# Second score product of the 64-wide heads over all 128 rows of the array

## The chip, the cores and the metric

The kernel runs on one core of one Trainium2 chip. The metric is the device time of one execution in microseconds. TensorE (PE, with its weight loads listed apart as PEld), VectorE (DVE), ScalarE (ACT), GpSimd (POOL) and SyncE (SP, which issues the transfers) each run their own instructions in order and wait for one another through semaphores.

## What is computed

The reference is two blocks on 256 tokens of width 1024. The first block has two layers; each layer norms latents and context, projects them with one wide matrix, runs three attention branches and sums them with gates. The second block has four mixers and is not touched here. What matters are the scores of two of the branches, whose heads are 64 wide:

```python
def diff_attend(q, k, v, lam):
    s = jnp.einsum('bqhmd,bkhmd->bhmqk', q * (DIFF_HD ** -0.5), k)
    p = jax.nn.softmax(s.astype(jnp.float32), axis=-1)
    a = (p[:, :, 0] - lam * p[:, :, 1]).astype(v.dtype)
    return jnp.einsum('bhqk,bkhd->bqhd', a, v)
...
def swa_context(q, k, v, sink):
    ...
    (p,) = sink_softmax(sink, (jnp.einsum('bqhgd,bkhd->bhgqk', qg, k),))
```

The differential branch has 8 heads of two 64-wide maps each, the sliding-window branch 16 heads of 64. All in float32.

## The kernel before, in words

Every float32 operand of a product is cut into two parts, a first (high) part and a second (low) part that is the rest, and a product is the sum of three matmuls: high by high, high by low, low by high (`mm3`, lines 101 to 103, most of the kernel's matmuls). The 64-wide heads use a shorter way. `pairs` (line 661) turns a query tile into one tile per half of the 128 partitions: the half that holds the head has its high part, the other half its low part. `twice` (line 673) does the keys: the high part of a head stands on both halves of a tile, and one more tile, `lo`, holds the low parts, each on its own half alone. So `scores` makes one score tile from two matmuls: line 850 over all 128 rows (high by high and low by high at once), and line 854 over the 64 rows of the head (high by low). Between them, for the sliding window's latents, line 853 adds the mask by a matmul with the identity. The heads of the differential branch get their keys from `twice` in `heads_t` (lines 646 to 659: four transposes into a PSUM bank of the kind `tp`, of which there are two), the first head of a unit while the unit before it is still in attention, the second head at the start of `diff_att`. The sliding window's keys already stand twice in the tile (`swa_keys`), so that `parts` gives both parts on both halves.

A layer runs its three branches in units of 256 columns, four to a branch; the projections of the next unit (many matmuls of lines 101 to 103) are put between the attention steps of a unit. The order on each engine is set by a scheduler at build time, from priorities by program order, and the slots of a pool are given out by it as they come free. The tiles of `pairs`, `twice` and the values are all of the kind `ut`, which has 12 buffers in the first layer and 15 in the second.

After the scores the row maximum is taken on DVE (lines 877 and 879), the exponential on ACT (line 882), the scaling on DVE (line 894), the turning on PE (line 903), and the product with the values on PE (lines 919 and 994).

Of the kernel before, what the change touches and what calls it, by code (L numbers as in the profile page):

```python
# [19 lines left out]
F32 = mybir.dt.float32  # L20
# [8 lines left out]
# Buffers of a kind: of the weights as loaded and in parts, of PSUM's banks, and of the first block's tiles  # L29
# by layer. Tiles of a kind are given out in the order of the program.  # L30
BUFS = dict(raw=3, w=4, start=12, mm=3, sc=2, tp=2, av=1, ut=(12, 15), yb=(26, 40), sz=4, pe=4, pt=2, st=2, tmp=2)
# How far ahead of their place in the program (or, if less than nothing, behind it) instructions are scheduled
# [3 lines left out]
class Core:  # L36
    """Buffers and the steps that every layer uses."""
# [28 lines left out]
    @contextmanager  # L66
    def shifted(self, ahead):
        """Instructions that are scheduled ahead of their place, and leave the others' as it is"""
        at = self.tc.cur_priority
        self.tc.cur_priority = max(0, at - ahead)  # L70
        yield
        self.tc.cur_priority = at

    # ---- float32 as the exact sum of two float32r parts
# [4 lines left out]
    def weights(self, src, k, f, stream=None):  # L79
        """A chunk of weights as granules [128, k, f], each with its two parts."""  # L80
        return [self.granule(src[g], k, f, stream) for g in range(src.shape[0])]
# [13 lines left out]
    def mm3(self, out, a, b, start, stop, ahead=False):  # L95
        """out += a.T @ b, with a and b as pairs of parts."""
        nc, tc = self.nc, self.tc
        at = tc.cur_priority
        if ahead:
            tc.cur_priority = max(0, at - AHEAD)  # L100
        nc.tensor.matmul(out, a[0], b[0], start=start, stop=False)  # L101
        nc.tensor.matmul(out, a[0], b[1], start=False, stop=False)  # L102
        nc.tensor.matmul(out, a[1], b[0], start=False, stop=stop)  # L103
        if ahead:
            tc.cur_priority = at + 3

    def gemm_n(self, out, h, cols, grans, k0=0, start=True, stop=True):
        """out [tokens, features]: the tokens' columns of h held, the weights moved."""
        ks = [(hi[:, k, :], lo[:, k, :]) for hi, lo in grans for k in range(hi.shape[1])]
        for k, w in enumerate(ks):  # L110
            a = (h[0][:, k0 + k, cols], h[1][:, k0 + k, cols])
            self.mm3(out, a, w, start and k == 0, stop and k == len(ks) - 1, True)

    def gemm_2(self, out, a, grans):
        """out += a.T @ weights, for columns of a that hold whole numbers or parts of them"""
        tc, nc = self.tc, self.nc
        ks = [g[i][:, k, :] for g in grans for k in range(4) for i in range(2)]
        at = tc.cur_priority
        for j, w in enumerate(ks):
            tc.cur_priority = max(0, at + j - AHEAD)  # L120
            nc.tensor.matmul(out, a[:, j // 2], w, start=j == 0, stop=j == len(ks) - 1)  # L121
        tc.cur_priority = at + len(ks)

    def gemm_t(self, out, gran, h, cols, k0=0, start=True, stop=True):
        """out [features, tokens]: the weights held, the tokens moved."""
        hi, lo = gran
        n = hi.shape[1]
# [4 lines left out]
    def rstd(self, pool, ss, n, name="rstd"):  # L132
        """(sum + n eps) ** -0.5: the root of n is left to the gain."""
        w = ss.shape[1]
# [10 lines left out]
    # ---- rows of tokens: their mean squares by blocks, and what is normed from them  # L145
    def squares(self, x, ss, i, width=256):
        """ss[:, i] = the sum of the squares of a block of x, over 1024"""
# [10 lines left out]
    def norm_turn(self, pool, xg, r, shift, h, cols_of, second=None):  # L158
        """h[:, k, cols] = parts of (xg r + shift).T, with the gain already in xg, but for the second
        half where its rows and gain are given"""  # L160
# [32 lines left out]
def silu2(c, work, p, shape_like=None, bufs=2):  # L193
    """2 silu(z) of z in PSUM, [128, n]."""
# [8 lines left out]
def out_gemm(c, x, w, yT, nk, gain):  # L203
    """x[t] += (y @ w) / 2; with the next norm's gain, the rows times it and their roots"""
# [107 lines left out]
def mixer_b(c, x, rs, P, i):  # L312
    nc = c.nc
    with ExitStack() as st:
        h = normed(c, rs, i)
        work = st.enter_context(c.pool(f"wb{i}", bufs=2))
        # gains: as columns past the rotary part, in the rotary tables within it
# [186 lines left out]
# ---- layouts on the host  # L504
def pack_k(np, w, f=256):
    """w [K, N], f columns at a time, cut along K: [N // f, K // 128 / k, 128, k, f], f k = 1024."""
# [5 lines left out]
def pack_f(np, w):  # L512
    """w [K, N], 256 columns at a time, cut along N: [N // 256, 2, 128, K // 128, 128]."""
# [50 lines left out]
class Hybrid:  # L564
    """A layer of the first block. Token tiles 0, 1 are latents and 2, 3 context."""
# [11 lines left out]
    def setup(self, pool, work):  # L577
        """Small tables of the layer."""
# [47 lines left out]
    def gemm_pair(self, grans, grp, n):  # L626
        """[128, 2, n] of the two token tiles of a group."""
# [6 lines left out]
    # ---- rotary: rows of heads [128, 2, heads, 2 * half]  # L634
# [11 lines left out]
    # ---- heads: parts of the transposes of stages [128, 2, width] by group  # L646
# [14 lines left out]
    def pairs(self, p, n):  # L661
        """For each half of the rows of p, its two parts as the halves of the rows of one tile: the
        number's own half has its first part, the other half the second."""
# [9 lines left out]
    def twice(self, p, n):  # L673
        """For each half of the rows of p, its first part on both halves of a tile; and the second parts."""
        nc = self.c.nc
        out = []
        lo = self.ut()
        for own, other in HALVES:
            t = self.ut()
# [3 lines left out]
            out.append(t)  # L683
        return out, lo

    # ---- latent attention
    def mla_prep(self):
# [7 lines left out]
        def rows(n):  # L695
            """Rows of the two token tiles of a group, and the sums of the squares of their parts"""
# [21 lines left out]
        def turned(src, grp, dst, gain, nk):  # L718
            """transposes with the gain, in parts"""
# [49 lines left out]
    def mla_proj(self, un):  # L769
        """Keys [nope | rotary twice] and queries [nope | x cos | x turned sin] of two heads, turned; the  # L770
        rotary part comes first in the second head."""
# [54 lines left out]
    def z_unit(self, r, un):  # L826
        """2 silu(z) of 256 columns, turned: two tiles [128, nt]"""
# [12 lines left out]
    def scores(self, p, q, k, half, grp, t, keys, mask=False):  # L840
        """q and k as parts; for a half q as tiles from pairs, and k's first part on both halves"""
# [6 lines left out]
        else:  # L848
            rows = HALVES[half][0]
# [4 lines left out]
            nc.tensor.matmul(p, q[half][rows, qs], k[1][rows, ks], start=False, stop=True)  # L854

    def softmaxes(self, q, k, half, grp, neg=None, sink=None):
        """Rows of probabilities [128, keys] of the group's two tiles; with neg, their negative
        lambda-fold factors besides, and not scaled."""
# [8 lines left out]
    def softmax(self, q, k, half, grp, ts, keys, neg, sink):  # L867
        """of tiles that share a bank"""
# [28 lines left out]
    def turned_p(self, ps, kts):  # L897
        """Parts of the transposes of two rows of probabilities, at two key tiles: [128 keys, 2, 256]"""
# [11 lines left out]
    def apply(self, out, ps, keys, v, both=None):  # L910
        """out [dv, 256 queries] = (p @ v).T"""
# [9 lines left out]
    def y_out(self, av, sz, col=None):  # L921
        """The branch's y silu(z) (twice), turned, in parts."""
# [12 lines left out]
    # ---- differential attention  # L935
    def qk_stage(self, gr, grp, heads, q, name):
        """[128, 2, heads * 64] after the rotation; the queries scaled."""
# [81 lines left out]
    # ---- sliding window  # L1019
    def swa_keys(self, su):  # L1020
        """Keys of two groups of heads, each twice, for the two halves of the partitions; and values, as their
        two parts side by side."""
# [20 lines left out]
        return [(((hi, hi), lo), v) for (hi, lo), v in zip(kt, vt)]  # L1043
# [10 lines left out]
    def swa_att(self, un, made, ahead):  # L1054
        """and what ahead() makes between its halves"""
# [23 lines left out]
    # ---- sum over the branches  # L1079
    def gates(self, r, dd, tile):  # L1080
        """tanh of half the gates"""
# [11 lines left out]
    def merge(self, r, parts):  # L1093
        """Parts of 256 columns of the sum over the branches; the last branch leaves its parts."""
# [31 lines left out]
    def run(self, K, h):  # L1126
        """The three branches, four units each; a unit's projections come before the attention of the one
        before it is through, and the sum over a branch goes along with the next one."""
# [30 lines left out]
# The parts of the sum over the branches that follow a branch's first units, by layer  # L1159
MERGE = (((0, 1, 2, 3),), ((0,), (1,), (2,), (3,)))  # L1160
# The steps of the modulation that go along with a branch's sum, by layer
# [5 lines left out]
class ModStart:  # L1167
    """The first layer's gain and shift, 256 columns at a time, for the rows of load_mixed: the latents'
    on the first half of the partitions, the context's on the others."""
# [23 lines left out]
class ModRows:  # L1193
    """Rows of the modulation, for the latents and the context, kept in DRAM: shift, gain with the
    norm's, and a quarter of the gate, for the two halves left out of silu and sigmoid."""
# [5 lines left out]
    def step(self, l, i, cc):  # L1201
        """256 columns of part i of layer l"""
# [19 lines left out]
    def row(self, l, i, pool, both):  # L1222
        """The row on all partitions, or the latents' on half of them and the context's on the others"""
# [7 lines left out]
def hybrid_out(c, P, l, xs, m, G, pool, xg, gain, done, first=None):  # L1231
    """xs += gate (merged @ w_out), xg = xs times the gain, and done(t, mean squares by blocks) as a
    tile is; with the gain after that, xs is times the gain (and done has its mean squares) and xg
    times both."""
# [29 lines left out]
def load_mixed(c, xp, P):  # L1264
    """Four tiles, each of 64 latents and 64 rows of context."""
# [6 lines left out]
def first_block(c, stack, P):  # L1272
    """The latents' rows, normed, as two tiles, and the sums of their squares."""
# [5 lines left out]
    with ExitStack() as st:  # L1279
# [60 lines left out]
        for l in range(2):  # L1340
# [8 lines left out]
            with c.pool(f"merged{l}", bufs=1, side="right") as mp:  # L1349
# [5 lines left out]
                with c.pool(f"tail{l}", bufs=1) as w:  # L1355
# [11 lines left out]
                    else:  # L1367
# [5 lines left out]
                        def done(t, ss, s2):  # L1373
                            """The two norms' roots: 1 / sqrt(s2 / (ss + eps) + eps) / sqrt(ss + eps)"""
# [106 lines left out]
```

## Time and profile before

| | us |
|---|---|
| median of 3 runs | 2538.19 |
| lowest and highest | 2535.25, 2541.75 |
| the profiled execution, span | 2537.5 |
| PE busy in it | 2494.2 |
| DVE, ACT, POOL busy | 1724.8, 1294.1, 155.7 |

The page gives each engine's busy time; a matmul's record has a modelled end, and matmuls overlap, so the length of a record says little of what it costs the engine. The start of a matmul to the start of the next one is what the engine spends on it. A row of the timeline gives start and length in us, the engine, the line, the tiles as out<-in and a form: "128\*128" is rows by columns of the array in use, "128x512" the partitions and columns that are moved through.

### The profile page before, as it was taken

To read this page: it belongs to the slowest core of one execution; us is meant where nothing else is said; L and a number is where in the kernel's file an instruction comes from. 1 tells how busy PE (TensorE), PEld (TensorE's weight loads), DVE (VectorE), ACT (ScalarE), POOL (GpSimd) and SP (SyncE) were. 2 spreads that over 40 slices of the span, in tenths; PEclk is the share of its full clock that TensorE was granted. 3 is DMA by queue.
4 is the path that set the end of the run, shared out by engine and by line. 5 is a ranking of instruction groups with operands and counts; after the bars stand their busy time and mean duration, and the time that the engine had idled before them with its cause. 6 is when DMAs were issued, how large, how long until landed. Compare 5 with 4: busy or idle time off the path is not lost.

```text
span 2537.5 us, 43544 instructions
## 1 busy us (share of the span) xinstructions
PE 2494.2 (98%) x17352; PEld 2276.2 (90%) x17352; DVE 1724.8 (68%) x3073; ACT 1294.1 (51%) x2566; POOL 155.7 (6%) x162
## 2 busy tenths in 40 slices
PE   9999999999999989999999999999999999999999
PEld 7889888888888868999999999999889998898998
DVE  4675655677747864686777888667667776685675
ACT  3554544555535553464555667454455555454643
POOL 0000011000010100210000000010000000000000
PEclk9999999999999999999999999999999999999999
DMA  6222244221232114323333433565554454455554
GB/s 251 77 71 67 63 139 149 67 67 50 84 122 71 58 50 148 102 92 100 117 117 117 142 101 116 200 192 174 167 180 149 152 156 132 158 183 192 175 168 148
DMA packets 91149, 321.40 MB, mean 127 GB/s; under 512 B 11641, under 2 KB 12481, under 8 KB 90945
## 3 DMA queue, kind: packets, MB, share of 16 engines
q1 hardware_dynamic: 90946, 318.62, 38.8%
q8 instruction: 136, 2.23, 0.4%
q14 instruction: 67, 0.55, 0.1%
HBM read 316.45 MB, written 2.13 MB: 126 GB/s over the span
## 4 chain that ended last, share of the span: by engine, by line
PE 95%; DVE 2%; ACT 1%; DMA 1%; issue 0%; POOL 0%; SPq 0%; ACTq 0%; POOLq 0%; DVEq 0%
PE mm L101 25%; PE mm L103 25%; PE mm L102 25%; PE sc L854 3%; PE tp L903 3%; PE av L919 3%; PE sc L850 2%; PE av L994 1%; PE mm L1188 1%; PE mm L121 1%; PE sc L103 1%; PE sc L102 1%; PE sc L101 1%; PE tp L653 1%; DVE wlo L77 1%; ACT whi L76 1%
## 5 line engine op out<-in xcount | busy, mean ns | idle before, releaser
L77 DVE TENSOR_TENSOR wlo<-raw,whi 128x1024 fp32r<-128x1024 f32 (+1 forms) x564 | 687.1, 1220 | 362.4 <-ACT whi L76 357.0
L76 ACT CAST whi<-raw 128x1024 fp32r<-128x1024 f32 (+1 forms) x564 | 586.6, 1043 | 664.7 <-PE mm L102 346.3
L101 PE MATMUL mm<-whi,hhi 128*128 128x256 f32 x2016 | 578.8, 288 | 4.1 <-ACT hhi L76 3.3
L103 PE MATMUL mm<-whi,hlo 128*128 128x256 f32 x2016 | 577.8, 288 | 2.0 <-DVE bgc L321 1.0
L102 PE MATMUL mm<-wlo,hhi 128*128 128x256 f32 x2016 | 575.5, 286 | 0.0
L103 PE MATMUL mm<-hhi,wlo 128*128 128x256 f32 (+1 forms) x1608 | 501.2, 313 | 0.0
L102 PE MATMUL mm<-hlo,whi 128*128 128x256 f32 (+1 forms) x1608 | 500.3, 312 | 0.0
L101 PE MATMUL mm<-hhi,whi 128*128 128x256 f32 (+1 forms) x1608 | 499.6, 312 | 0.0
L101 PEld LDWEIGHTS mm<-whi,hhi 128*128 128x128 f32 x2016 | 386.4, 192 | 11.5 <-ACT hhi L76 4.3
L103 PEld LDWEIGHTS mm<-whi,hlo 128*128 128x128 f32 x2016 | 385.2, 191 | 11.9 <-issue 8.3
L102 PEld LDWEIGHTS mm<-wlo,hhi 128*128 128x128 f32 x2016 | 386.5, 192 | 6.3 <-issue 5.1
L102 PEld LDWEIGHTS mm<-hlo,whi 128*128 128x128 f32 x1608 | 307.3, 191 | 16.6 <-issue 2.0
L103 PEld LDWEIGHTS mm<-hhi,wlo 128*128 128x128 f32 x1608 | 307.3, 191 | 16.6 <-issue 1.5
L101 PEld LDWEIGHTS mm<-hhi,whi 128*128 128x128 f32 x1608 | 307.1, 191 | 16.0 <-issue 1.2
L882 ACT ACTIVATE pe<-sc,sst 128x512 f32<-128x512 f32 (+1 forms) x240 | 147.5, 617 | 122.4 <-DVE sst L877 75.4
L101 PE MATMUL mm<-yb,whi 128*128 128x512 f32 (+1 forms) x440 | 152.3, 349 | 4.7 <-ACT yb L76 3.7
L102 PE MATMUL mm<-yb,whi 128*128 128x512 f32 (+1 forms) x440 | 151.7, 345 | 0.8 <-DVE yb L77 0.8
L103 PE MATMUL mm<-yb,wlo 128*128 128x512 f32 (+1 forms) x440 | 151.4, 344 | 0.0
L77 DVE TENSOR_TENSOR ptl<-tp,pth 128x512 fp32r<-128x512 f32 x160 | 108.0, 684 | 27.2 <-ACT pth L76 18.3
L76 ACT CAST pth<-tp 128x512 fp32r<-128x512 f32 x160 | 91.1, 587 | 63.9 <-PE tp L903 51.4
L877 DVE TENSOR_REDUCE sst<-sc 128x1 f32<-128x512 f32 (+1 forms) x120 | 81.8, 686 | 46.3 <-PE sc L854 32.2
L903 PE MATMUL tp<-ident,pe 128*128 128x128 f32 x640 | 102.1, 275 | 0.8 <-DVE ptl L77 0.8
(320 smaller groups left out, 4081.1 us busy)
## 6 DMA issues: line engine op xcount, KB each, us to landing
raw<-in_b_qkv_dram SPq DMA_DIRECT2D x72, 512.0 KB
raw<-in_a_uz_dram SPq DMA_DIRECT2D x64, 512.0 KB
raw<-in_win_z_dram SPq DMA_DIRECT2D x48, 512.0 KB
raw<-in_win_d_dram SPq DMA_DIRECT2D x48, 512.0 KB
raw<-in_win_g_dram SPq DMA_DIRECT2D x48, 512.0 KB
raw<-in_wbr_dram SPq DMA_DIRECT2D x48, 512.0 KB
raw<-in_w_mod_dram SPq DMA_DIRECT2D x32, 512.0 KB
raw<-in_a_v_dram SPq DMA_DIRECT2D x32, 512.0 KB
```

The lines of the kernel that those rows point to most:

```text
L76: self.nc.scalar.copy(hi, src)
L77: self.nc.vector.tensor_sub(lo, src, hi.bitcast(F32))
L101: nc.tensor.matmul(out, a[0], b[0], start=start, stop=False)
L102: nc.tensor.matmul(out, a[0], b[1], start=False, stop=False)
L103: nc.tensor.matmul(out, a[1], b[0], start=False, stop=stop)
L121: nc.tensor.matmul(out, a[:, j // 2], w, start=j == 0, stop=j == len(ks) - 1)
L850: nc.tensor.matmul(p, q[half][:, qs], k[0][half][:, ks], start=True, stop=False)
L854: nc.tensor.matmul(p, q[half][rows, qs], k[1][rows, ks], start=False, stop=True)
L877: nc.vector.tensor_reduce(st[:, 0], p, axis=AX, op=OP.max, negate=True)
L882: nc.scalar.activation(e[:, i], p[:, i], AF.Exp, bias=st[:, 0, i:i + 1], accum_out=st[:, 1, i:i + 1])
L903: nc.tensor.transpose(p[:, i * 256 + t * 128:i * 256 + t * 128 + 128], ps[t][:, kt * 128:kt * 128 + 128], c.ident)
L919: c.nc.tensor.matmul(out, w, p, start=lo + j + i == 0, stop=lo == 1 and j == nk - 1)
```

## The change

`twice` now makes a low-part tile for each half, as it already did for the high part: the low part on its own half as before (DVE, line 682), and a copy of it on the other half by GpSimd. It returns two lists. `scores` makes the second product over all 128 rows, from the same query tile as the first, and the caller of the sliding window passes its low-part tile for both halves. With the query's low part on the other half the second product now adds low by low as well. Comments and docstrings are taken out, which moves the lines below by two.

```diff
     def twice(self, p, n):
...
         nc = self.c.nc
-        out = []
-        lo = self.ut()
+        his, los = [], []
         for own, other in HALVES:
-            t = self.ut()
+            t, lo = self.ut(), self.ut()
             nc.scalar.copy(t[own, :n], p[own, :n])
             nc.scalar.copy(t[other, :n], t[own, :n].bitcast(F32))
             nc.vector.tensor_sub(lo[own, :n], p[own, :n], t[own, :n].bitcast(F32))
-            out.append(t)
-        return out, lo
+            nc.gpsimd.tensor_copy(lo[other, :n], lo[own, :n].bitcast(F32))
+            his.append(t)
+            los.append(lo)
+        return his, los
...
         else:
-            rows = HALVES[half][0]
             nc.tensor.matmul(p, q[half][:, qs], k[0][half][:, ks], start=True, stop=False)
             if mask:
                 o = p[:, 128:256] if t == 0 else p[:, 0:128]
                 nc.tensor.matmul(o, self.K["ident"], self.K["swa_mask"][:, t], start=False, stop=False)
-            nc.tensor.matmul(p, q[half][rows, qs], k[1][rows, ks], start=False, stop=True)
+            nc.tensor.matmul(p, q[half][:, qs], k[1][half][:, ks], start=False, stop=True)
...
-        return [(((hi, hi), lo), v) for (hi, lo), v in zip(kt, vt)]
+        return [(((hi, hi), (lo, lo)), v) for (hi, lo), v in zip(kt, vt)]
```

The scheduler moves instructions by a few places. Three places matter below. First TensorE, at the first scores of the first differential unit of layer 0 (`tp` is the bank of the turned keys, `sc` the scores, `ut` the tiles of queries and keys, `mm` the projection of the unit that follows). Before:

```order
L653 MATMUL tp_2682<-ident_61,st_k_2292 128x128
L653 MATMUL tp_2682<-ident_61,st_k_2292 128x128
L653 MATMUL tp_2682<-ident_61,st_k_2347 128x128 x2
L850 MATMUL sc_2709<-ut_2595,ut_2608 128x512
L854 MATMUL sc_2709<-ut_2594,ut_2608 128x512
L103 MATMUL mm_2974<-whi_2969,hlo_80 128x256
```

and after the change:

```order
L653 MATMUL tp_2685<-ident_61,st_k_2292 128x128
L653 MATMUL tp_2685<-ident_61,st_k_2292 128x128
L653 MATMUL tp_2685<-ident_61,st_k_2347 128x128 x2
L852 MATMUL sc_2715<-ut_2594,ut_2611 128x512
L856 MATMUL sc_2715<-ut_2595,ut_2611 128x512
L102 MATMUL mm_2980<-wlo_2970,hhi_79 128x256
```

The sequence is the same, four matmuls earlier; the two score matmuls still stand side by side, with projection matmuls behind them.

Second VectorE, in the same unit, where the low parts of the second head's two key tiles are made (line 682; 669 is the same step of its queries). Before, both stand between the first two row maxima:

```order
L877 TENSOR_REDUCE sst_2711<-sc_2709 128x1
L682 TENSOR_TENSOR ut_2687<-tp_2682,ut_2688 64x512
L877 TENSOR_REDUCE sst_2720<-sc_2718 128x1
L886 RECIPROCAL sst_2711<-sst_2711 128x1
L682 TENSOR_TENSOR ut_2687<-tp_2682,ut_2692 64x512
```

After, the first stands there still, and the second is here, 16 rows further on:

```order
L986 SCALAR_TENSOR_TENSOR pe_2735<-pe_2744,sst_2745,pe_2735 128x512
L879 TENSOR_REDUCE sst_2794<-sc_2792 128x2
L682 TENSOR_TENSOR ut_2697<-tp_2685,ut_2696 64x512
L669 TENSOR_TENSOR ut_2707<-tp_2702,ut_2707 64x512
L879 TENSOR_REDUCE sst_2807<-sc_2805 128x2
```

It now stands one row ahead of the first of the two L669 of the same head, which has kept its place; the scheduler had a `ut` slot for it only there.

Third GpSimd, at the start of the differential branch (L789 are copies for the branch before, `dr` a root of the branch's norm, `modrow` a row of the modulation). Before:

```order
L789 CAST ut_1917<-km0_428 64x512
L789 CAST ut_1918<-km1_429 64x512
L142 TENSOR_TENSOR dr_3415<-dre_3413,mhalf_70 128x8
L1213 TENSOR_TENSOR modrow_3606<-modrow_3606,modlow_3609 2x256
L1213 TENSOR_TENSOR modrow_3645<-modrow_3645,modlow_3648 2x256
```

and after:

```order
L791 CAST ut_1917<-km0_428 64x512
L791 CAST ut_1918<-km1_429 64x512
L683 CAST ut_2595<-ut_2595 64x512
L683 CAST ut_2601<-ut_2601 64x512
L683 CAST ut_2691<-ut_2691 64x512
L683 CAST ut_2697<-ut_2697 64x512
L142 TENSOR_TENSOR dr_3424<-dre_3422,mhalf_70 128x8
L683 CAST ut_3332<-ut_3332 64x512
L683 CAST ut_3338<-ut_3338 64x512
L1215 TENSOR_TENSOR modrow_3615<-modrow_3615,modlow_3618 2x256
```

The new copies (L683) stand in units of two ahead of and behind the roots; there are 32 in the program. The order of the transfers on SyncE is the same as before.

## Rows read from the trace of the kernel before

**Rows 1.** The page: span, engines (busy, share, instructions), the chain that ended last by engine.

```profile
span 2537.5 us, 43544 instructions
...
PE 2494.2 (98%) x17352; PEld 2276.2 (90%) x17352; DVE 1724.8 (68%) x3073; ACT 1294.1 (51%) x2566; POOL 155.7 (6%) x162
...
PE 95%; DVE 2%; ACT 1%; DMA 1%; issue 0%; POOL 0%; SPq 0%; ACTq 0%; POOLq 0%; DVEq 0%
```

**Rows 2.** Line 854 alone: duration ns min/median/max, first and last start, forms.

```profile
L854 PE MATMUL sc<-ut x192: 377/492/793, 259.1 to 1577.6; 64*128 64x512 f32 x128, 64*128 64x256 f32 x64
```

**Rows 3.** Weight loads by line: busy us, mean ns of one | idle us before them.

```profile
L850 PEld LDWEIGHTS sc<-ut 128*128 128x128 f32 x192 | 36.6, 191 | 8.6 <-issue 2.7 <-ACT pe L882 1.0
...
L854 PEld LDWEIGHTS sc<-ut 64*128 64x128 f32 x192 | 35.2, 183 | 36.2 <-issue 27.9
...
L853 PEld LDWEIGHTS sc<-swm,idr 128*128 128x128 f32 x64 | 12.2, 191 | 0.4
```

**Rows 4.** Timeline of PE (start us, us, engine, line), full-row matmuls of 512 columns.

```profile
902.41 0.40 PE L102 MATMUL mm<-yb,whi 128*128 128x512 f32 x1
...
903.34 0.40 PE L103 MATMUL mm<-yb,wlo 128*128 128x512 f32 x1
```

**Rows 5.** Timeline of PE, a differential score of 512 keys.

```profile
276.75 0.40 PE L850 MATMUL sc<-ut 128*128 128x512 f32 x1
277.08 0.50 PE L854 MATMUL sc<-ut 64*128 64x512 f32 x1
277.51 0.38 PE L101 MATMUL mm<-whi,hhi 128*128 128x256 f32 x1
277.73 0.28 PE L102 MATMUL mm<-wlo,hhi 128*128 128x256 f32 x1
277.85 0.28 PE L103 MATMUL mm<-whi,hlo 128*128 128x256 f32 x1
```

**Rows 6.** Timeline of PE, a sliding-window score with its mask.

```profile
633.55 0.22 PE L853 MATMUL sc<-swm,idr 128*128 128x128 f32 x1
633.70 0.49 PE L854 MATMUL sc<-ut 64*128 64x512 f32 x1
634.12 0.38 PE L101 MATMUL mm<-whi,hhi 128*128 128x256 f32 x1
634.34 0.28 PE L102 MATMUL mm<-wlo,hhi 128*128 128x256 f32 x1
```

**Rows 7.** Timeline of PE, two scores of 256 keys (context rows).

```profile
270.13 0.28 PE L850 MATMUL sc<-ut 128*128 128x256 f32 x1
270.34 0.38 PE L854 MATMUL sc<-ut 64*128 64x256 f32 x1
270.65 0.39 PE L850 MATMUL sc<-ut 128*128 128x256 f32 x1
...
271.28 0.39 PE L102 MATMUL mm<-wlo,hhi 128*128 128x256 f32 x1
271.50 0.28 PE L103 MATMUL mm<-whi,hlo 128*128 128x256 f32 x1
```

**Rows 8.** GpSimd copies of 64x512 in the kernel before: duration ns min/median/max.

```profile
L789 POOL CAST ut<-km x24: 604/614/1298, 110.6 to 1131.5; 64x512 fp32r<-64x512 f32 x24
```

**Rows 9.** Timeline, a low part as made on DVE and its first use on PE.

```profile
1195.79 0.69 DVE L682 TENSOR_TENSOR ut<-tp,ut 64x512 fp32r<-64x512 f32 x1
...
1201.45 0.50 PE L854 MATMUL sc<-ut 64*128 64x512 f32 x1
```

**Rows 10.** Stretches: us, busy us of PE, PEld, DVE, ACT, POOL, then granted clock.

```profile
425.00:640.00 215.00, 215.00 (x1452) 187.63 (x1451) 155.36 (x323) 117.71 (x281) 6.94 (x4) 1.00 0.21 68
880.00:930.00 50.00, 44.06 (x225) 33.48 (x223) 37.09 (x92) 33.17 (x84) 2.58 (x2) 0.93 0.04 11
```

**Rows 11.** Line 854 from 880 to 930 us, columns as in Rows 2.

```profile
L854 PE MATMUL sc<-ut x15: 378/383/793, 881.5 to 919.2; 64*128 64x256 f32 x8, 64*128 64x512 f32 x7
```

**Rows 12.** Longest wait of PE from 860 to 930 us: total, times, longest.

```profile
PE av L919 <- DVE dos L1071: 1.7, 1, 1.7
```

## The prediction

> **What bounds the kernel now.** I read the page first, to see which engine sets the end: PE is busy for 98% of the span, and the chain that ended last runs through PE for 95% of it, while VectorE stands at 68% and ScalarE at 51% [rows 1]. So time that a change takes off PE's own sequence comes off the span, except where PE waits for others. Then the view of line 854, for how many matmuls are changed and when they run: 192, of which 128 move 512 columns and 64 move 256, all between 259 and 1578 us [rows 2]. Then the weight loads by line: the full-row load of line 850 has 8.6 us of idle time before its 192 instances (0.045 us each), the half-row load of line 854 has 36.2 us (0.19 us each), most of it under "issue", so PE waited for no other engine [rows 3]. That made me look at what a half-row matmul costs its neighbours, in the timeline, by starts.
>
> **What the half rows cost.** Full-row matmuls of 512 columns that follow each other start every 0.2325 us (four steps from 902.41 to 903.34) [rows 4], those of 256 columns every 0.12 us (277.73 to 277.85) [rows 5]. Around a half-row matmul the steps are longer, in three places: from the matmul ahead of it, from itself to the next, and from that next one to the one behind it. I take the three patterns that make up the 192, each from the start of the first matmul ahead to the start of the second one behind, and put the full-row pace in place of it.
>
> Differential, 512 keys, 64 of them (128 less the 64 with a mask, counted by the loads of line 853 [rows 3]): 276.75 to 277.73 is 0.98 us [rows 5]. At full-row pace it would be 0.2325 + 0.2325 + 0.12 = 0.585. Saved 0.395, times 64 = 25.3 us.
>
> Sliding window with mask, 64 of them: from the mask at 633.55 to 634.34 is 0.79 us [rows 6]. At full-row pace 0.2325 + 0.12, and the mask's own step. No row shows a mask followed by a full-row matmul, so its step has bounds: 0.15, what it takes now [rows 6], and 0.06, half of the 256-column step [rows 5]. Saved 0.29 to 0.38; I take 0.33, between the two, since nothing here tells which is nearer. Times 64 = 21 us (18.4 to 24.1).
>
> 256 keys, 64 of them, in 32 pairs of two: 270.13 to 271.50 is 1.37 us for five steps [rows 7], at 0.12 each 0.60. Saved 0.77 a pair, times 32 = 24.6 us.
>
> Together 71 us, 68 to 74 by the bounds of the mask. The mechanism that I read from this: with the array's rows set differently, the weights of the next matmul are not loaded while the one before runs, once into the half and once back out of it, and the step behind that is late as well. A full-row second product has nothing of it.
>
> Against this, full-row loads might be thought to be the dear ones. In the trace a load of 128 rows takes 0.19 us (36.6 us over 192 [rows 3]) and yet full-row matmuls start 0.12 us apart [rows 5], so the load lies beside another matmul. The Trainium skill, page "TensorE: Matmul & The Clock Gate", section "The mechanism", says the opposite, that a weight load goes beside a running matmul only where the row groups differ. By that rule the change would leave the load of the second product exposed and gain nothing, 2538; by the rows it gains the 71. The trace of this kernel disagrees with the rule, and I go by the rows.
>
> **What the change adds.** 32 copies on GpSimd, 64 by 512 (16 calls of `twice`, two halves each). The nearest rows are the same engine's copies of the same shape: 0.61 us at the median, 1.30 at most [rows 8], so 20 us in all, at most 42, on an engine that is busy for 156 of 2537 us [rows 1]. None lies on the path: each low part is used no sooner than some 5 us after it is made. The shortest such stretch in the trace runs from 1195.79 + 0.69 = 1196.48 to 1201.45 [rows 9], 5.0 us, and the copy wants 0.61 to 1.30 of that. Ahead of the copies in GpSimd's queue stand the roots `dr` and the `modrow` steps, which are over by then in the order shown; behind the copies wait those same steps, each later by two copies at most, 1.2 us, and they feed tiles for the end of a unit or rows that are read much later. If this cover were gone, one exposed copy would cost 0.61 to 1.30 us, 32 of them 20 to 42 us. VectorE and ScalarE get no further instruction, and PE has the same number of matmuls, and the transfers keep their order.
>
> It also takes one more `ut` tile per call, 16 instead of 14 for a unit, of 12 or 15 buffers. In the order this shows at one place: the second low part of the second head has moved back by 16 rows on VectorE, to just ahead of the first L669 of the same head. Both query tiles of that head end on L669, behind it in either order, so its scores waited for those before, and they stand at about the same place on PE. I cost it at nothing, with L669 as its cover; without it, PE would wait there eight times, by the rival below.
>
> **What is not kept.** Where PE waits for others, a shorter sequence on PE only makes the wait longer. The last unit of layer 0 is such a place, since no projection is left to fill in: from 880 to 930 PE is busy for 44.1 of 50 us and the granted clock is 0.93 [rows 10]; 15 of the 192 lie in it [rows 11], and the longest wait is 1.7 us for VectorE [rows 12]. The 15 are worth 15 x 0.37 = 5.5 us by the mean of the sum (71 / 192), and I give back half, 3 us. From 425 to 640 PE is busy without a break and VectorE for 155 of 215 us, 72% [rows 10]; even 30 us off PE there, more than that stretch's share of the 71 by time, would raise VectorE to 155 of 185, 84%, which still leaves PE the bound; so only small waits, 1 us in all. So 71 - 3 - 1 = 67 us are left: 2537.5 - 67 = 2470.5 by the profiled execution, which lies 0.7 us under the median of the runs, so **2471 us**. Its own range is 2462 (74 kept, and a little more where the clock no longer falls to 1.2 GHz) to 2484 (the low bound 68, less 14 given back).
>
> **Rivals.** *Part of it is given back:* softmax steps on VectorE and ScalarE become the bound in the attention stretches, so that about half is kept. For it: VectorE's 72% is an average, and between a score and its transposes PE needs VectorE twice. Against it: no idle time of PE from 425 to 640 [rows 10]. 20 to 50 us kept: 2488 to 2518.
>
> *No gain:* the long steps belong to the second product as such (it loads the same query columns again) and not to its 64 rows. For it: only this line shows them. Against it: full-row matmuls of lines 101 and 102 load the same columns twice too, and keep 0.2325 us [rows 4]. 2538.
>
> *More than that:* the steps at full rows are shorter still, or stretches at the lower of the two clock levels fall away. 80 us saved: 2458.
>
> *Slower:* the `ut` slots. The second low part of a second head gets its slot late, and the bank of turned keys is held until then, so PE, which runs in order, stands in front of the next turning or score, once in each of the eight units. It turns the sign once a stop is over 67 / 8 = 8.4 us; at 10 us it gives 2471 + 80 = 2551. For it: 16 tiles on 12 buffers, and the move in the order. Against it: the move ends ahead of an L669 that both kernels wait for.
>
> **How the numbers follow.** Forecast 0.73, part of it 0.12, no gain 0.06, more 0.05, slower 0.04. About 0.3% is what a measurement of this kernel can tell from no change. Forecast, part and more are all faster by over 0.3%: 0.90; no gain is within it: 0.06; slower 0.04. For 8 in 10 the range takes in the forecast, the case of more down to 2458, and the nearer part of the second case, up to 2500.
>
> **What would show it.** In the profile after: the second product as 128*128, 192 of them; 850 to 856 in 0.23 us at 512 columns and 0.12 at 256; idle time before its weight load near that of line 850 in [rows 3] instead of 36 us; PE's gaps behind it gone. Nearly all of the gain between 259 and 1578 us, the second block unchanged. It would be wrong if the steps stay long, if waits for GpSimd appear in front of the second product, or if PE waits for DVE in stretches where it did not before.

## The result and the profile after

The changed kernel takes 2470.41 us (median of 4 runs, 2469.18 to 2472.44) against 2538.75 of the kernel before beside it: a ratio of 0.9734, 95% interval 0.972 to 0.9747. The forecast was 2471.

The page of the kernel after, in the parts that answer to [rows 1]: span, engines, and the chain that ended last.

```profile
span 2468.8 us, 43646 instructions
...
PE 2423.8 (98%) x17352; PEld 2269.2 (92%) x17352; DVE 1723.5 (70%) x3073; ACT 1292.0 (52%) x2566; POOL 179.7 (7%) x194
...
PE 94%; DVE 2%; ACT 1%; DMA 1%; issue 0%; POOL 0%; SPq 0%; ACTq 0%; POOLq 0%; DVEq 0%
```

PE's busy time has fallen by 70.4 us, from 2494.2 to 2423.8, and the span by 68.7, from 2537.5 to 2468.8. PE still has 98% of the span and most of the chain; it has the same 17352 matmuls. GpSimd has 32 instructions and 24.0 us more, the copies. The last second product starts at 1510.0 us (below) instead of 1577.6 [rows 2], 67.6 us earlier, so nearly all of the gain is made by then and the second block adds next to nothing.

The second product by its line, now 856, as in [rows 2] (duration ns min/median/max, first and last start, forms):

```profile
L856 PEld LDWEIGHTS sc<-ut x192: 187/188/331, 259.6 to 1510.0; 128*128 128x128 f32 x192
L856 PE MATMUL sc<-ut x192: 274/395/736, 259.8 to 1510.0; 128*128 128x512 f32 x128, 128*128 128x256 f32 x64
```

All 192 run at 128\*128. The weight loads by line (busy us, mean ns | idle us before), which answer to [rows 3]:

```profile
L852 PEld LDWEIGHTS sc<-ut 128*128 128x128 f32 x192 | 36.8, 192 | 2.5 <-ACT pe L884 1.6
...
L856 PEld LDWEIGHTS sc<-ut 128*128 128x128 f32 x192 | 36.5, 190 | 2.9
```

The idle time ahead of the second product's loads has gone from 36.2 us to 2.9, and ahead of the first product's from 8.6 to 2.5. The first fell too: in the kernel before, 44 of the loads of line 850 came directly behind a half-row one, as in [rows 7], and 6.9 of the 8.6 us stood ahead of these.

The timeline of PE, for the differential score as in [rows 5], then for a score with its mask as in [rows 6] (here with matmuls of 512 columns behind it):

```profile
275.76 0.39 PE L852 MATMUL sc<-ut 128*128 128x512 f32 x1
275.99 0.40 PE L856 MATMUL sc<-ut 128*128 128x512 f32 x1
276.22 0.28 PE L102 MATMUL mm<-wlo,hhi 128*128 128x256 f32 x1
276.34 0.28 PE L103 MATMUL mm<-whi,hlo 128*128 128x256 f32 x1
...
626.31 0.40 PE L852 MATMUL sc<-ut 128*128 128x512 f32 x1
626.55 0.22 PE L855 MATMUL sc<-swm,idr 128*128 128x128 f32 x1
626.61 0.45 PE L856 MATMUL sc<-ut 128*128 128x512 f32 x1
626.89 0.40 PE L103 MATMUL mm<-hhi,wlo 128*128 128x512 f32 x1
```

Line 852 to 856 is 0.23 us, 856 to the next 0.23, and the one behind that 0.12: from 275.76 to 276.34 it is 0.58 us where [rows 5] had 0.98. With the mask, 626.55 to 626.89 is 0.34 us: 0.06 for the mask's step and 0.28 for the second product's. Two scores of 256 keys, as in [rows 7]:

```profile
271.27 0.28 PE L852 MATMUL sc<-ut 128*128 128x256 f32 x1
271.39 0.28 PE L856 MATMUL sc<-ut 128*128 128x256 f32 x1
271.50 0.28 PE L852 MATMUL sc<-ut 128*128 128x256 f32 x1
271.62 0.28 PE L856 MATMUL sc<-ut 128*128 128x256 f32 x1
271.74 0.28 PE L102 MATMUL mm<-wlo,hhi 128*128 128x256 f32 x1
271.85 0.28 PE L103 MATMUL mm<-whi,hlo 128*128 128x256 f32 x1
```

From 271.27 to 271.85 it is 0.58 us for the five steps; it was 1.37.

Where the weight loads stand in time shows what has gone. First the loads of the second product and of the matmul behind it in the kernel before, around the score of [rows 5] (the bracket is the idle time ahead of a load and what ended it), then the same two loads after:

```profile
277.08 0.18 PEld L854 LDWEIGHTS sc<-ut 64*128 64x128 f32 x1 [0.25 <-issue]
277.51 0.19 PEld L101 LDWEIGHTS mm<-whi,hhi 128*128 128x128 f32 x1 [0.25 <-issue]
...
275.76 0.19 PEld L856 LDWEIGHTS sc<-ut 128*128 128x128 f32 x1
275.99 0.19 PEld L102 LDWEIGHTS mm<-wlo,hhi 128*128 128x128 f32 x1
```

Before, both loads start where the record of their own matmul starts (277.08 and 277.51 [rows 5]), after 0.25 us of idle time. After, each starts with the matmul ahead of its own (275.76 and 275.99) and lies beside it.

The copies on GpSimd (durations, then what ended GpSimd's idle time before them: us, times):

```profile
L683 POOL CAST ut<-ut x32: 603/612/2267, 253.1 to 1329.4; 64x512 fp32r<-64x512 f32 x32
...
  DVE ut L682: 248.7, 28
```

They take 0.61 us at the median, as their neighbours did [rows 8]; three took 2.13 to 2.27, each straight behind `modrow` steps. GpSimd mostly waited for their sources, and the list of PE's waits has none for GpSimd.

### The profile page after: what moved, and what is told of

It reads as the page before. It is cut to its first block, busy times and chain, and to the rows that moved or that the text cites. A ratio compares the mean times of both kernels' runs of the same rounds, so it can differ in the third digit from the quotient of the medians.

```text
span 2468.8 us, 43646 instructions
## 1 busy us (share of the span) xinstructions
PE 2423.8 (98%) x17352; PEld 2269.2 (92%) x17352; DVE 1723.5 (70%) x3073; ACT 1292.0 (52%) x2566; POOL 179.7 (7%) x194
## 3 DMA queue, kind: packets, MB, share of 16 engines
HBM read 316.45 MB, written 2.13 MB: 129 GB/s over the span
## 4 chain that ended last, share of the span: by engine, by line
PE 94%; DVE 2%; ACT 1%; DMA 1%; issue 0%; POOL 0%; SPq 0%; ACTq 0%; POOLq 0%; DVEq 0%
PE mm L101 25%; PE mm L102 25%; PE mm L103 25%; PE tp L905 3%; PE av L921 3%; PE sc L856 2%; PE sc L852 1%; PE av L996 1%; PE mm L1190 1%; PE mm L121 1%; PE sc L103 1%; PE sc L102 1%; PE sc L101 1%; PE tp L653 1%; DVE wlo L77 1%; ACT whi L76 1%
## 5 line engine op out<-in xcount | busy, mean ns | idle before, releaser
L76 ACT CAST pth<-tp 128x512 fp32r<-128x512 f32 x160 | 91.2, 587 | 49.7 <-PE tp L905 40.8
L101 PEld LDWEIGHTS mm<-yb,whi 128*128 128x128 f32 x440 | 84.0, 192 | 15.4 <-ACT yb L76 4.1
```

Source lines behind the costliest of these rows:

```text
L76: self.nc.scalar.copy(hi, src)
```

## The experiments

Seven kernels were run, each in the same rounds as the kernel before. A change of rows is meant below as a place in PE's order where a matmul over 64 rows follows one over 128, or the other way round.

**The sliding window alone.** From the kernel before, in `scores` and `swa_keys`:

```diff
-            nc.tensor.matmul(p, q[half][rows, qs], k[1][rows, ks], start=False, stop=True)
+            if isinstance(k[1], tuple):
+                nc.tensor.matmul(p, q[half][:, qs], k[1][half][:, ks], start=False, stop=True)
+            else:
+                nc.tensor.matmul(p, q[half][rows, qs], k[1][rows, ks], start=False, stop=True)
...
-        return [(((hi, hi), lo), v) for (hi, lo), v in zip(kt, vt)]
+        return [(((hi, hi), (lo, lo)), v) for (hi, lo), v in zip(kt, vt)]
```

> The second product over 128 rows in the sliding window alone; the differential branch keeps 64 rows, its three ut tiles and no copy. My theory (each change between half and full rows costs PE its own time): 64 masked products save 0.33 us each and 16 pairs of 256 keys 0.77 a pair, 21.1 + 12.3 = 33 us of the 2538.75 of before, so 2505. Rival, the scheduler's new order or the differential branch carries the gain: nearly nothing here, 2530 to 2539.

Measured 2503.79 us against 2539.22, ratio 0.9865 (0.985 to 0.9879): 35 us off, 33 expected. Its weight loads by line, the second product of the sliding window (full rows, 855) and that of the differential branch (half rows, 857):

```profile
L855 PEld LDWEIGHTS sc<-ut 128*128 128x128 f32 x96 | 18.2, 190 | 2.6
...
L857 PEld LDWEIGHTS sc<-ut 64*128 64x128 f32 x96 | 17.6, 183 | 20.0 <-issue 15.8
```

The idle time stands ahead of the half-row loads alone, 20.0 us for 96, 2.6 for the other 96.

**The differential branch alone**, with its copies and its further tiles. From the changed kernel:

```diff
-            nc.tensor.matmul(p, q[half][:, qs], k[1][half][:, ks], start=False, stop=True)
+            rows = slice(0, 128) if isinstance(k[1], list) else HALVES[half][0]
+            nc.tensor.matmul(p, q[half][rows, qs], k[1][half][rows, ks], start=False, stop=True)
```

> The other part alone: copies, the further ut tiles and 128 rows in the differential branch, 64 rows in the sliding window. My theory: 64 products of 512 keys save 0.395 us each and 16 pairs of 256 keys 0.77 a pair, 25.3 + 12.3 = 38 us, so 2501; with the kernel that does the sliding window alone the two savings should add up to the 68 us of both. Rival, copies and slots cost something that the whole hid: above 2510, and the two would add up to less than 68 us.

Measured 2502.45 us against 2539.22, ratio 0.9858 (0.9841 to 0.9874): 37 us off, 38 expected. The two parts together are 35 + 37 = 72 us, against 68 to 69 for the whole; each interval is about 4 us to either side, so these runs do not tell 72 from 68. Neither part hides a cost of the other that can be seen.

**What is added, without what is taken away.** From the changed kernel, copies and tiles kept, each second product over the 64 rows of its head:

```diff
-            nc.tensor.matmul(p, q[half][:, qs], k[1][half][:, ks], start=False, stop=True)
+            rows = HALVES[half][0]
+            nc.tensor.matmul(p, q[half][rows, qs], k[1][half][rows, ks], start=False, stop=True)
```

> All that the change adds and nothing of what it takes away: four ut tiles per call of twice and the 32 copies on GpSimd, but each second product over 64 rows as before. My theory: copies and slots lie beside other work, 2538 within 4 us. Rival, slots: PE stands in front of the second heads, above 2545. Rival, the scheduler's moves make the gain: 2470 to 2500.

Measured 2537.47 us against 2539.22, ratio 0.9997 (0.9988 to 1.0006): no difference, within 3 us. Its half-row loads:

```profile
L857 PEld LDWEIGHTS sc<-ut 64*128 64x128 f32 x192 | 35.2, 183 | 36.2 <-issue 27.8
```

The 32 copies are there (0.61 us at the median), and the loads have the 36.2 us of idle time of [rows 3] again. The instructions stand in the order of the changed kernel: by line, operation and kind of tile, VectorE, ScalarE and GpSimd agree with it in every place and PE in all but 4 of 17352. So neither the copies, nor the further tile per call, nor the scheduler's moves are worth anything that can be measured, to either side; the rows of the second product are worth all of it.

**The copies on ScalarE.** From the changed kernel:

```diff
-            nc.gpsimd.tensor_copy(lo[other, :n], lo[own, :n].bitcast(F32))
+            nc.scalar.copy(lo[other, :n], lo[own, :n].bitcast(F32))
```

> The changed kernel with its 32 copies on ScalarE instead of GpSimd, at some 0.62 us each, so 20 us more on an engine at 52%, which stands ahead of the scores. My theory: 5 us of cover for each, so no difference, 2470 within 3 us. Rival, the copies are on the path where they are made: up to 32 x 0.62 = 20 us more, 2490.

Measured 2470.23 us, ratio to the kernel before 0.9735 (0.9719 to 0.9751), that of the changed kernel. Which of the two engines makes them does not matter here.

**Twice as many half-row matmuls, no further change of rows.** From the kernel before, for 512 keys:

```diff
-            nc.tensor.matmul(p, q[half][rows, qs], k[1][rows, ks], start=False, stop=True)
+            for o in range(0, n, 256):
+                nc.tensor.matmul(p[:, o:o + 256], q[half][rows, qs], k[1][rows, ks.start + o:ks.start + o + 256],
+                                 start=False, stop=o + 256 == n)
```

> The kernel before, with each second product of 512 keys made as two half-row matmuls of 256 columns, one behind the other: 128 half-row matmuls more, and no further change between half and full rows. My theory (the change of rows is what costs, not the half rows): the two take 2 x 0.12 in place of 0.2325, 128 x 0.01 = 1 us, so 2540. Rival, a half-row matmul is slow by itself, by the 0.19 us that its step is longer or by more: 128 x 0.19 to 0.31, so 2563 to 2579.

Measured 2540.91 us against 2537.83, ratio 1.0015 (1.0006 to 1.0025): 2 to 6 us more where 1 was expected, not 25 or more. The timeline of PE around one of them (x2 is the two half-row matmuls, now line 855), and all half-row loads of this kernel:

```profile
276.05 0.40 PE L850 MATMUL sc<-ut 128*128 128x512 f32 x1
276.38 0.50 PE L855 MATMUL sc<-ut 64*128 64x256 f32 x2
276.81 0.39 PE L101 MATMUL mm<-whi,hhi 128*128 128x256 f32 x1
277.04 0.28 PE L102 MATMUL mm<-wlo,hhi 128*128 128x256 f32 x1
...
L855 PEld LDWEIGHTS sc<-ut 64*128 64x128 f32 x320 | 50.1, 186 | 37.3 <-issue 29.1
```

The two take from 276.38 to 276.81, 0.43 us, what the single one took in [rows 5] (277.08 to 277.51), and the steps ahead of them and behind them are the same 0.33 and 0.23. A half-row matmul behind another costs what a full-row one does. The 320 loads have 37.3 us of idle time ahead of them where 192 had 36.2 [rows 3]; ahead of the 123 that come directly behind another half-row load there is none. The other 5 of the 128 were put apart by the scheduler, with full-row matmuls between them, so this kernel has 10 changes of rows more after all (403 against 393, counted in PE's order), which may be part of the 3 us.

**Fewer changes of rows with the same matmuls.** From the kernel before, for two scores of 256 keys in one bank, in the order full, full, half, half (in `scores`, left out here, `part` says which of the two products is made):

```diff
...
-        for i, t in enumerate(ts):
-            self.scores(p[:, i], q, k, half, grp, t, keys, sink is not None and grp == 0)
+        for part in ((0,), (1,)) if half is not None and m == 2 else ((0, 1),):
+            for i, t in enumerate(ts):
+                self.scores(p[:, i], q, k, half, grp, t, keys, sink is not None and grp == 0, part)
```

> The kernel before, with the two scores of 256 keys that share a bank made as full, full, half, half instead of full, half, full, half: the same matmuls, and two changes of rows instead of four in each of 32 pairs. My theory: a pair goes from 1.37 us to 0.12 + 0.21 + 0.12 + 0.31 + 0.22 = 0.98, so 32 x 0.39 = 12 us off, 2526. Rival, a half-row matmul is slow by itself: no difference, 2538.

Measured 2528.27 us against 2537.83, ratio 0.996 (0.9945 to 0.9974): 10 us off, 7 to 14 by the interval, 12 expected. One pair in its timeline (851 is the first product, 856 the second):

```profile
268.94 0.39 PE L851 MATMUL sc<-ut 128*128 128x256 f32 x2
269.26 0.50 PE L856 MATMUL sc<-ut 64*128 64x256 f32 x2
269.69 0.39 PE L102 MATMUL mm<-wlo,hhi 128*128 128x256 f32 x1
269.92 0.28 PE L103 MATMUL mm<-whi,hlo 128*128 128x256 f32 x1
```

From 268.94 to 269.92 it is 0.98 us, as worked out, instead of 1.37. The number of half-row matmuls is the same as before; what fell is the number of changes, by 60 in PE's order (from 393 to 333): 30 of the 32 pairs stand as wanted.

**Another matmul with half rows.** From the changed kernel, the mask over 64 rows, which leaves out the mask of the second 64 queries of each tile:

```diff
-                nc.tensor.matmul(o, self.K["ident"], self.K["swa_mask"][:, t], start=False, stop=False)
+                nc.tensor.matmul(o, self.K["ident"][:64], self.K["swa_mask"][:64, t], start=False, stop=False)
```

> The changed kernel, with the 64 mask matmuls of the sliding window over 64 rows instead of 128: this leaves out the mask of the second half of each tile's queries. It is another matmul, of 128 columns, between two that are full. My theory: each change of rows costs the same there, 0.10 ahead of it, 0.19 behind it and 0.10 one further on, 64 x 0.33 to 0.39, so 21 to 25 us more than the changed kernel, 2491 to 2495. Rival, only the second product of scores has the long steps (the same query columns loaded twice, half of them unused): 2470.

Measured 2490.84 us against 2537.83, ratio 0.9814 (0.9798 to 0.9831), so 20 us above the changed kernel's 2470.41, 21 to 25 expected. Its timeline (first product, mask, second product, the next), and the loads of the mask:

```profile
600.39 0.40 PE L852 MATMUL sc<-ut 128*128 128x512 f32 x1
600.72 0.33 PE L855 MATMUL sc<-swm,idr 64*128 64x128 f32 x1
600.98 0.50 PE L856 MATMUL sc<-ut 128*128 128x512 f32 x1
601.32 0.28 PE L103 MATMUL mm<-whi,hlo 128*128 128x256 f32 x1
...
L855 PEld LDWEIGHTS sc<-swm,idr 64*128 64x128 f32 x64 | 11.9, 186 | 17.5 <-issue 17.4
```

From 600.39 to 601.32 it is 0.93 us where the changed kernel takes 0.58 (626.31 to 626.89). A matmul of 128 columns of its own, which reads neither queries nor keys, brings the same long steps once its rows are half, and its loads the idle time (17.5 us for 64; over full rows, in the changed kernel, it was 0.7). So they do not belong to the second product of the scores.

## Why the prediction was right, point by point

**PE as the bound** held: 70.4 us off its busy time made 68.7 us off the span. The stretch from 425 to 640 us, which [rows 10] has of before, is now (us, busy us of PE, PEld, DVE, ACT, POOL, clock):

```profile
425.00:640.00 215.00, 215.00 (x1556) 201.93 (x1555) 171.38 (x366) 128.74 (x317) 15.47 (x15) 1.00 0.23 74
```

PE still has no break there, with VectorE at 171 of 215 us instead of 155.

**The three patterns.** The full-row pace came out as taken: 0.58 us for the differential score (0.585 taken), 0.58 for the five steps of two 256-key scores (0.60 taken). The mask, which no row of before showed between full-row matmuls, takes a step of 0.06 and leaves 0.28 for the second product, 0.34 together; the sum had taken the middle of its bounds, 0.105 + 0.2325 = 0.3375. That the mask's step was the lower bound and the two together still came out at the middle is luck: the mask's own step is as short as its columns, and the step behind it is longer by 0.05, which the sum did not have.

**The mechanism.** The sum of the two halves of the change, the kernel with twice the half-row matmuls, the regrouped one and the mask over 64 rows together show that the price hangs on each change between 64 and 128 rows and not on the half-row matmul, on the second product or on the order. Counted in PE's order, the kernel before has 393 changes of rows (9 of them at matmuls over one row), either half of the change alone 201, the whole only those 9, and the one with the half mask 137. By the medians that is 0.18 us a change for the whole, 0.18 and 0.19 for the halves and 0.16 for the mask and for the regrouped pairs; the 128 half-row matmuls more, nearly without a change, cost 3 us in all, 0.02 each. That PE does not load the next weights beside the matmul at such a change stands in the loads' own rows: in the kernel before 36.2 us of idle time ahead of the 192 loads into the half and 41.3 ahead of the 192 back out of it. What the engine does in that time is not shown.

**The copies and slots at nothing** held, and the kernel with copies alone shows it: 0.9997. Three copies took 2.13 to 2.27 us, above the 1.30 that I had as the bound, and began only when the `modrow` steps ahead of them were over, 0.5 to 0.7 us after the source was ready (1209.20 to 1209.74 for the longest), where I had those steps as over by then. The cover hid both, since PE waits for none of the copies.

**What is given back.** 3 us for the last unit of layer 0 and 1 us elsewhere. In that unit, from the first of its last 15 second products (881.53 before, 839.66 after, both by the timeline) to the first matmul of line 101 behind its last product with the values (931.26, 886.54) it is 49.7 us before and 46.9 after: 2.8 of the 5.5 us kept. These two stretches (columns as above), then PE's waits for other engines inside them, before and after (total us, times, longest):

```profile
881.53:931.26 49.73, 42.53 (x214) 32.19 (x213) 36.14 (x90) 32.71 (x82) 2.58 (x2) 0.93 0.04 11
839.66:886.54 46.88, 38.57 (x215) 31.66 (x213) 36.10 (x92) 32.24 (x82) 2.59 (x2) 0.92 0.04 12
```

```profile
PE av L919 <- DVE ptl L77: 1.4, 3, 1.0
PE tp L903 <- DVE ptl L77: 0.8, 1, 0.8
PE sc L850 <- ACT pe L882: 0.5, 1, 0.5
...
PE av L921 <- ACT pth L76: 1.7, 1, 1.7
PE av L921 <- DVE ptl L77: 1.5, 3, 1.1
PE tp L905 <- DVE sst L887: 1.2, 1, 1.2
PE sc L852 <- ACT pe L884: 0.8, 2, 0.6
```

PE's busy time fell by 4.0 us and the stretch by 2.8, so 1.1 us came back as longer waiting, on VectorE and ScalarE: with the 1.7 us of [rows 12] the waits listed are 4.4 us before and 5.2 after. The 2.8 us for the next step's input, at the end of each stretch, are the same in both. The granted clock is 0.93 before and 0.92 after, so stretches at 1.2 GHz did not fall away. On the whole 71 - 68.7 = 2.3 us were given back instead of 4, which is within what the runs differ by. For the same reason it is luck that the median came within 1 us of the forecast: the changed kernel's own runs lie 3 us apart.

**The rivals.** Part of it given back and no gain are out by the time, 68 us; the reason behind no gain, that the long steps belong to the second product, is out by the mask over 64 rows. Slower by the slots is out by the kernel with copies alone. More than that did not come: the steps at full rows are those of the sum. The Trainium skill's rule on weight loads ("TensorE: Matmul & The Clock Gate", section "The mechanism"), by which nothing would have been gained, is not borne out as the sentence "only when row_grp differs" has it: in the kernel after, the loads of scores and projections are over full rows, 0.19 us each, and matmuls of 256 columns start 0.12 us apart. The same section of the Trainium skill also lets a load into a "background weight buffer" go ahead, whatever its row group; that would fit the trace, but no run here shows which buffer a load goes to.

## What to carry to other kernels

Look at starts of matmuls, not at their lengths, and look at the two matmuls behind an odd one as well as at the one ahead of it. A matmul over 64 rows in a stream of 128-row ones cost 0.33 to 0.40 us more than its columns here; filling the other half with something useful cost nothing on PE, and GpSimd or ScalarE had the time to write it. Where half rows have to stay, put them side by side; in both runs that did so the neighbours were on the same half of the array, and two different halves side by side were not run.

## What was not expected

A change in the number of columns in use, from 128 to 34, has no such price. In the kernel after, matmuls of line 121 use 34 columns of the array, next to full ones of line 102:

```profile
362.22 0.40 PE L102 MATMUL mm<-yb,whi 128*128 128x512 f32 x1
362.46 0.28 PE L121 MATMUL mm<-whi,silu 128*34 128x256 f32 x1
362.57 0.28 PE L121 MATMUL mm<-wlo,silu 128*34 128x256 f32 x1
...
364.09 0.28 PE L121 MATMUL mm<-whi,silu 128*34 128x256 f32 x1
364.21 0.40 PE L103 MATMUL mm<-yb,wlo 128*128 128x512 f32 x1
```

From a full 512-column matmul to the first of 34 columns it is 0.24 us, 0.11 from there to the next, and 0.12 from the last back to a full one, the pace of full ones.

The mask shows one more thing: its step is 0.06 us, and the step behind it 0.28 instead of 0.2325. I read this as a matmul of 128 columns being too short to cover the weight load of the one behind it, which takes 0.19 us; no run was made to test that.
